# A hybrid decoder layer on one core: V projected 512 columns at a time, with a new opening

## The chip, the core and the metric

The kernel runs on one core of one Trainium2 chip. Time is device time in microseconds of that core, from the launch to the end of one execution; lower is better. The engines are TensorE (PE; its weight loads are PEld), VectorE (DVE), ScalarE (ACT), GpSimd (POOL) and SyncE (SP, which here only issues transfers). Transfers are issued from the queues of SP, ACT and POOL.

## The reference

One layer, with x of 1024 tokens by 1024 columns in float32. `h` is the RMS-normalised x; one wide product gives q, k, v (1024 columns each), u (2048) and the gates g (2048).

```python
h = rms_norm(x, attn_norm_w)
q, k, v, u, g = jnp.split(h @ w_in, splits, axis=-1)
# branch A: differential attention, 8 heads, q and k normalised, T5 bias, causal
y_a = (rms_norm(diff_attention(...), subln_w) * (1 - lam_init)) @ w_proj_attn
# branch B: GLU, causal depthwise convolution of width 31, LayerNorm, silu
c = causal_depthwise_conv(u_a * sigmoid(u_b), conv_w, conv_b)
y_b = silu(layer_norm(c, conv_ln_w, conv_ln_b)) @ w_proj_conv
x = x + (sigmoid(g_a + gate_b_a) * y_a + sigmoid(g_b + gate_b_b) * y_b) @ w_out
h = rms_norm(x, ffn_norm_w)
gt, up = jnp.split(h @ w_gate_up, 2, axis=-1)
x = x + (silu(gt) * up) @ w_down
```

## The kernel before

Every float32 operand of a large product is split into a high part (a cast on ACT, `split_hi`, L119) and a low part (a subtraction on DVE, `split_lo`, L124). A product is then three matmuls, high by high, high by low, low by high (`mm3`, L152 to L154).

**Opening.** x comes in eight tiles of 128 tokens (`xload`, L167, four buffers). The norm weights are broadcast to 128 partitions by a transfer on ACT's queue (L173). Small vectors (convolution bias, layer-norm weights, gate bias, norm weights of q and k, convolution weights, the four lambda vectors) are loaded from POOL's queue, turned by TensorE into columns of `pvec` and `cw`, and scaled (L175 to L230). `xtile` (L622) normalises one tile through `norm_T` (L606): a Square with a running sum on ACT, a reciprocal root in several small DVE operations, two multiplies of 512 columns, eight transposes on TensorE into `px`, and casts and subtractions into `hT_hi` and `hT_lo`, the transposed normalised x that all projections read.

**First phase.** The list `first` names blocks: `V` (256 columns of v), `U` (128 columns of both halves of u) and `Q` (a head's q and k). `run` asks each block's generator for one step after the other. `v_item` (L633) keeps a token tile as the stationary operand and streams 256 weight columns (`gemm_N`); two token tiles fill one bank of 512 columns, which is split and stored. In the first V block it also calls `xtile` for every tile. `u_item` (L539) keeps 128 weight columns stationary and streams 512 tokens (`gemm_T`); its four steps end in stores of the gated u. Weights are taken from a stream, `ws`, which runs two loads ahead; a raw load (`wraw`, two buffers) is split into `whi` and `wlo` (three buffers).

**Taps.** When a U block is complete, its 31 convolution taps on DVE (L519, L525) join the list `bg`. Each step of the first phase hands out 3.25 entries of that list (`TAPS_FIRST`); those that remain are spread over the 64 steps of attention, by the slack that a formula gives each step. Attention also carries the remaining Q and all G blocks on TensorE. Later stages (projections, output, the feed-forward part) are not touched.

**Order.** The program is traced in the order of the code, and a scheduler then fixes each engine's order before the launch by a simulated timeline. `after(ins)` puts the instructions of a block behind `ins` on the engine of `ins`.

Of the kernel before, what the change touches and what calls it, by code (L numbers as in the profile page):

```python
# [2 lines left out]

# [53 lines left out]
def kernel(  # L57
# [107 lines left out]
    xts = {}  # L165

    def xload(i):  # L167
        xts[i] = ap.tile([P, D], F32, tag="xt", name=f"xt{i}", bufs=4)
        nc.sync.dma_start(xts[i][:], xs[i * P : (i + 1) * P, :])

    xload(0)
    wb = ap.tile([P, D], F32, name="anw_b", bufs=1)
    nc.scalar.dma_start(wb[:], attn_norm_w.to_broadcast([P, D]))  # L173

    NROW = 64  # L175
    rows = ap.tile([NROW, P], F32, name="rows", bufs=1)
    pool.memset(rows[:], 0.0)
    col = {}
    at = [0]

    def vec_rows(key, src, n):
        r0 = at[0]
        pool.dma_start(rows[r0 : r0 + n, :], src.rearrange("o (k p) -> (o k) p", p=P))
        col[key] = r0
        at[0] += n

    vec_rows("conv_b", conv_b, 8)
    vec_rows("ln_w", conv_ln_w, 8)
    vec_rows("ln_b", conv_ln_b, 8)
    vec_rows("gate_b", gate_b, 16)  # L190
    vec_rows("subln", subln_w, 1)
    for key, src in (("qn", q_norm_w), ("kn", k_norm_w)):
        r0 = at[0]
        for j in range(2):
            pool.dma_start(rows[r0 : r0 + 1, j * HD : (j + 1) * HD], src)
        col[key] = r0
        at[0] += 1
    pvec = cst.tile([P, NROW], F32, name="pvec")
    pt = pm()
    pe.transpose(pt[:, :NROW], rows[:], ident[:NROW, :NROW])  # L200
    dve.tensor_copy(pvec[:], pt[:, :NROW])

    def pcol(key, k=0):
        c = col[key] + k
        return pvec[:, c : c + 1]

    dve.tensor_scalar(pcol("subln"), pcol("subln"), 1.0 - LAM_INIT, None, op0=ALU.mult)
    dve.tensor_scalar(pcol("kn"), pcol("kn"), -(HD ** -0.5), None, op0=ALU.mult)
    c_ = col["ln_w"]
    dve.tensor_scalar(pvec[:, c_ : c_ + 8], pvec[:, c_ : c_ + 8], -0.125, None, op0=ALU.mult)  # L210

    cwrow = ap.tile([CW, D], F32, name="cwrow", bufs=1)
    pool.dma_start(cwrow[:], conv_w[0])
    cw = cst.tile([P, NKT, 32], F32, name="cw")
    pt = pm()
    for k in range(NKT):
        pe.transpose(pt[:, k * 32 : k * 32 + CW], cwrow[:, k * P : (k + 1) * P], ident[:CW, :CW])
    dve.tensor_copy(
        cw[:, :, :CW], pt[:, : NKT * 32].rearrange("p (k t) -> p k t", t=32)[:, :, :CW]
    )  # L220

    lamt = ap.tile([P, 4, HD], F32, name="lamt", bufs=1)
    for j, src in enumerate((lam_q1, lam_k1, lam_q2, lam_k2)):
        pool.dma_start(lamt[:, j, :], src.to_broadcast([P, HD]))
    neglam = cst.tile([P, 1], F32, name="neglam")
    lprod = ap.tile([P, 2, HD], F32, name="lprod", bufs=1)
    lsum = cst.tile([P, 2], F32, name="lsum")
    for j in range(2):
        dve.tensor_tensor(lprod[:, j, :], lamt[:, 2 * j, :], lamt[:, 2 * j + 1, :], op=ALU.mult)
    dve.tensor_reduce(lsum[:], lprod[:], axis=AX.X, op=ALU.add)  # L230
# [75 lines left out]

    ws = Stream(2)

    def kt(m, k):
        return m[k] if isinstance(m, list) else m[:, k, :]  # L310

# [18 lines left out]
    v_hi = [dr.tile([S, 256], F32, name=f"v_hi{j}") for j in range(4)]  # L330
    v_lo = [dr.tile([S, 256], F32, name=f"v_lo{j}") for j in range(4)]
# [36 lines left out]

    for it in first + [x_ for l_ in later for x_ in l_]:
# [6 lines left out]
    def ld_pair(w, k, c):  # L376


        def go():
            raw = wraw()  # L380
            nc.sync.dma_start(
                raw[:].rearrange("p (k c) -> p k c", c=512),
                w[k * P : (k + 2) * P, 512 * c : 512 * (c + 1)].rearrange("(k p) c -> p k c", p=P),
            )
            hi, lo = wsplit(raw)
            return hi[:].rearrange("p (k c) -> p k c", c=512), lo[:].rearrange("p (k c) -> p k c", c=512)

        return go


    WO = ((0, (0, 1)), (1, (0,)), (1, (1,)))
    for c, _ in WO:
        ws.plan([ld_pair(wout, k, c) for k in range(0, NKT, 2)])

# [119 lines left out]
    def conv_taps(c):  # L514
# [17 lines left out]

        return [first_tap] + [tap(t) for t in range(1, CW)]

    hT_hi = big.tile([P, NKT, S], F32R, tag="xhi", name="hT_hi")
    hT_lo = big.tile([P, NKT, S], F32R, tag="xlo", name="hT_lo")


    def u_item(c):  # L539
        wb_, wa_ = ws.next(), ws.next()  # L540
        for sb in range(2):
            cs = slice(sb * 512, (sb + 1) * 512)
            ob = gemm_T(wb_, hT_hi, hT_lo, sb)
            sg = wp.tile([P, 512], F32, tag="sg", name=nm("sg"), bufs=2)
            act.activation(sg[:], ob[:], AF.Sigmoid)
            yield
            oa = gemm_T(wa_, hT_hi, hT_lo, sb)
            dve.tensor_tensor(sg[:], oa[:], sg[:], op=ALU.mult)
            nc.sync.dma_start(u_d[c][:, cs], sg[:])
            if sb == 1:  # L550
                bg.todo.insert(max(0, len(bg.todo) - CW), conv_load(c))
                bg.add(conv_taps(c))
            yield
# [52 lines left out]
    def norm_T(src, wb, hi, lo, i, junk, hbuf, tp, rstd):  # L606

        ss = sm.tile([P, 1], F32, tag="ss", name=nm("ss"))
        act.activation(junk, src, AF.Square, accum_out=ss[:])
        r = rstd(ss[:], 1.0 / D)  # L610
        for g in range(2):
            half, gs = hbuf(g), slice(512 * g, 512 * (g + 1))
            dve.scalar_tensor_tensor(half, src[:, gs], r, wb[:, gs], op0=ALU.mult, op1=ALU.mult)
# [16 lines left out]
            lambda ss, scale: rstd_of(ss, 1, scale),  # L630
        )

    def v_item(j):  # L633
        if j == 0:
            xtile(0)
        halves = [ws.next(), ws.next()]
        if j == 0:
            for i in range(1, 4):
                xload(i)
        for i2 in range(NT // 2):  # L640
            o = pg()
            for e in range(2):
                i = 2 * i2 + e
                if j == 0:
                    if i:
                        xtile(i)
                    if i + 4 < NT:
                        xload(i + 4)
                gemm_N(o[:, 256 * e : 256 * (e + 1)], halves, hT_hi, hT_lo, i)
            vh = ap.tile([P, 512], F32R, tag="vh", name=nm("vh"))  # L650
            vl = ap.tile([P, 512], F32R, tag="vl", name=nm("vl"))
            split_hi(vh[:], o[:])
            split_lo(vl[:], o[:], vh[:])
            for src, dst in ((vh, v_hi[j]), (vl, v_lo[j])):
                nc.sync.dma_start(
                    dst[256 * i2 : 256 * (i2 + 1), :].rearrange("(e p) c -> p e c", p=P),
                    f32(src[:]).rearrange("p (e c) -> p e c", c=256),
                )
            yield

    def bias_rows():
# [15 lines left out]
        pool.dma_start(t_d[h][:], b_d[h : h + 1, :].to_broadcast([P, TL]))  # L677

    qk_ctx = ExitStack()
    qkp = qk_ctx.enter_context(tc.tile_pool(name="qkp", bufs=2, side="right", reuse_waits="tile"))  # L680
    T = {}
    late = []

    def q_item(h):
        halves = [ws.next(), ws.next()]
        t = {}
        T[h] = t
# [56 lines left out]
    def run(items):  # L744
        for it in items:
            gen = MAKE[it[0]](int(it[1:]))
            while True:
# [5 lines left out]
                        late.pop(0)[1]()  # L753
                yield

    n = 0
# [25 lines left out]
    def load_v(h):  # L782
        vh = aps.tile([P, NT, VD], F32R, tag="vh", name=f"vh{h}", bufs=1)
        vl = aps.tile([P, NT, VD], F32R, tag="vl", name=f"vl{h}", bufs=1)
        for dst, src in ((vh, v_hi[h // 2]), (vl, v_lo[h // 2])):
            nc.sync.dma_start(
                f32(dst[:]),
                src[:, (h % 2) * VD : (h % 2 + 1) * VD].rearrange("(k p) d -> p k d", p=P),
            )
        V[h] = vh, vl  # L790

# [729 lines left out]
```

## Time and profile before

| | |
|---|---|
| median of three runs | 1765.96 us (1763.79 to 1766.74) |
| the profiled execution | 1767.11 us, span 1765.3 us |
| granted TensorE clock, mean | 0.998 |
| TensorE busy | 1742.3 us (99%) |
| VectorE busy | 1272.9 us (72%) |
| ScalarE busy | 801.1 us (45%) |
| first transpose of x on TensorE | at 9.35 us |
| first V block, 256-column matmuls | 11.11 us on |

Times of instructions come from the profiled execution and count from the start of its span. In a line of the profile `L152` is a line of the kernel, `out<-in` are the names of the tiles, `x64` is a count, and after `|` stand busy time in microseconds, the mean duration of one in nanoseconds, and the idle time of the engine before it with what ended it. Matmuls overlap, so their durations add up to more than the time they take. `SPq` and `ACTq` are the transfer-issuing sides of the engines.

### The profile page before, as it was taken

How to read it: one execution, taken by the hardware profiler on the slowest of the kernel's cores; microseconds unless marked ns; L12 is line 12 of the kernel's file. 1: busy time of each engine (PE TensorE's matmuls, PEld its weight loads, DVE VectorE, ACT ScalarE, POOL GpSimd, SP SyncE). 2: the span in 40 equal slices, each digit the busy share in tenths (PEclk: the TensorE clock that was granted, in tenths of full speed). 3: DMA queues.
4: the chain of work that ended last, by engine and by line, in shares of the span. 5: the costliest groups of instructions: out<-in, count | busy, mean ns of one | idle time of the engine just before them, and what ended most of it. 6: DMA issues, size and time to landing. Idle time of an engine off the chain costs nothing.

```text
span 1765.3 us, 25836 instructions
## 1 busy us (share of the span) xinstructions
PE 1742.3 (99%) x9367; PEld 1503.9 (85%) x9367; DVE 1272.9 (72%) x2187; ACT 801.1 (45%) x1886; POOL 26.6 (2%) x106
## 2 busy tenths in 40 slices
PE   7999999999999999999999999999999999999999
PEld 5898998998999998988888888878888888888887
DVE  6388888999988898886787525867667666665544
ACT  4211241558767776755557313633333333333332
POOL 3000000000000000000000000000000000000000
PEclk9999999999999999999999999999999999999999
DMA  7533354235444344352983444234544544697663
GB/s 213 197 114 110 118 143 138 72 99 147 112 134 128 90 114 142 90 159 72 338 269 103 167 167 144 90 94 157 172 150 156 178 155 140 204 355 249 215 217 130
DMA packets 255728, 275.34 MB, mean 156 GB/s; under 512 B 16064, under 2 KB 177896, under 8 KB 255600
## 3 DMA queue, kind: packets, MB, share of 16 engines
q1 hardware_dynamic: 253568, 267.45, 47.4%
q0 software_dynamic: 1744, 5.19, 1.0%
q8 instruction: 74, 1.21, 0.3%
q10 hardware_dynamic: 288, 1.05, 0.2%
q14 instruction: 54, 0.44, 0.1%
HBM read 176.59 MB, written 78.68 MB: 145 GB/s over the span
## 4 chain that ended last, share of the span: by engine, by line
PE 93%; DMA 3%; DVE 2%; ACT 1%; issue 1%; SPq 0%; DVEq 0%; ACTq 0%
PE acc L1375 19%; PE pg L152 15%; PE pg L154 15%; PE pg L153 15%; PE acc L451 12%; PE sc L817 2%; PE sc L816 2%; PE wo L154 2%; PE wo L152 2%; PE wo L153 2%; PE pT L852 2%; PE pW L152 1%; PE pW L154 1%; PE pW L153 1%; DMA xt<-in_x_dram 1%; PE pQ L714 1%
## 5 line engine op out<-in xcount | busy, mean ns | idle before, releaser
L525 DVE SCALAR_TENSOR_TENSOR acc<-u,cw,acc 128x1024 f32<-128x1024 f32 x240 | 307.1, 1280 | 2.8
L152 PE MATMUL pg<-whi,hT_hi 128*128 128x256 f32 x768 | 220.8, 288 | 0.7 <-ACT hT_hi L119 0.6
L154 PE MATMUL pg<-whi,hT_lo 128*128 128x256 f32 x768 | 220.2, 287 | 0.5 <-DVE hT_lo L124 0.2
L153 PE MATMUL pg<-wlo,hT_hi 128*128 128x256 f32 x768 | 219.5, 286 | 0.4 <-DVE wlo L124 0.4
L119 ACT CAST whi<-wraw 128x1024 fp32r<-128x1024 f32 x109 | 114.4, 1050 | 215.6 <-PE pg L153 121.5
L152 PE MATMUL pg<-hT_hi,whi 128*128 128x512 f32 x512 | 201.7, 394 | 0.0
L154 PE MATMUL pg<-hT_hi,wlo 128*128 128x512 f32 x512 | 201.0, 393 | 0.0
L153 PE MATMUL pg<-hT_lo,whi 128*128 128x512 f32 x512 | 200.6, 392 | 0.0
L124 DVE TENSOR_TENSOR wlo<-wraw,whi 128x1024 fp32r<-128x1024 f32 x109 | 133.1, 1222 | 71.0 <-ACT whi L119 66.9
L124 DVE TENSOR_TENSOR wlo<-draw,whi 128x1024 fp32r<-128x1024 f32 x75 | 91.8, 1225 | 89.3 <-ACT whi L119 84.8
L152 PEld LDWEIGHTS pg<-whi,hT_hi 128*128 128x128 f32 x768 | 148.0, 193 | 3.8 <-ACT hT_hi L119 1.4
L154 PEld LDWEIGHTS pg<-whi,hT_lo 128*128 128x128 f32 x768 | 148.0, 193 | 2.4 <-DVE hT_lo L124 0.7
L153 PEld LDWEIGHTS pg<-wlo,hT_hi 128*128 128x128 f32 x768 | 148.1, 193 | 2.2 <-DVE wlo L124 0.7
L119 ACT CAST whi<-draw 128x1024 fp32r<-128x1024 f32 x75 | 78.8, 1051 | 129.8 <-PE acc L451 119.6
L451 PE MATMUL acc<-wlo,whi 128*128 128x512 f32 x308 | 119.9, 389 | 0.0
L451 PE MATMUL acc<-whi,wlo 128*128 128x512 f32 x308 | 119.8, 389 | 0.0
L823 ACT ACTIVATE E<-E,mn 128x256 f32<-128x256 f32 (+7 forms) x128 | 99.8, 780 | 35.9 <-DVE mn L818 33.7
L154 PEld LDWEIGHTS pg<-hT_hi,wlo 128*128 128x128 f32 x512 | 96.2, 188 | 19.1
L153 PEld LDWEIGHTS pg<-hT_lo,whi 128*128 128x128 f32 x512 | 96.3, 188 | 18.5
L152 PEld LDWEIGHTS pg<-hT_hi,whi 128*128 128x128 f32 x512 | 96.3, 188 | 18.3
L1375 PE MATMUL acc<-h_lo,whi 128*128 128x512 f32 x240 | 93.4, 389 | 0.0
L1375 PE MATMUL acc<-h_hi,whi 128*128 128x512 f32 x240 | 93.4, 389 | 0.0
(270 smaller groups left out, 3957.0 us busy)
## 6 DMA issues: line engine op xcount, KB each, us to landing
wraw<-in_w_gate_up_dram SPq DMA_DIRECT2D x44, 512.0 KB, 4.8
wraw<-in_w_in_dram SPq DMA_DIRECT2D x40, 512.0 KB, 4.5
qs<-qs SPq DMA_DIRECT2D x96, 128.0 KB, 2.3
wd<-in_w_down_dram SPq DMA_DIRECT2D x44, 256.0 KB, 3.1
tdT<-wd SPq DMA_DIRECT2D x88, 128.0 KB, 4.4
draw<-sdS SPq DMA_DIRECT2D x44, 256.0 KB, 3.8
draw<-tdT SPq DMA_DIRECT2D x44, 256.0 KB, 3.7
wraw<-in_w_in_dram SPq DMA_DIRECT2D x32, 256.0 KB, 3.3
```

Of the source, the lines that this page charges most:

```text
L119: act.copy(dst, src)
L124: last_lo[0] = dve.tensor_tensor(dst, src, f32(hi), op=ALU.subtract).ins
L152: pe.matmul(o, lh, rh, start=start, stop=False)
L153: pe.matmul(o, lh, rl, start=False, stop=False)
L154: last_mm[0] = pe.matmul(o, ll, rh, start=False, stop=stop).ins
L451: m = pe.matmul(o[s_][i][:], l_[:, ts], r_[:, 512:], start=start and j + y_ == 0, stop=j == n - 1 and y_ == 2, skip_group_check=not start,)
L525: dve.scalar_tensor_tensor(acc[0][:], us[c][:, t : t + S], cw[:, c, t : t + 1], acc[0][:], op0=ALU.mult, op1=ALU.add)
L816: pe.matmul(o[:, :w], qh[:, qs], k, start=True, stop=False)
L817: last_mm[0] = pe.matmul(o[:, :w], ql[:, qs], k, start=False, stop=True).ins
L823: act.activation(e[:, :nk], e[:, :nk], AF.Exp, bias=mn[:, j : j + 1], scale=-1.0, accum_out=l[:, j : j + 1])
L852: pe.transpose(pt[:, k * P : (k + 1) * P], e[:, (k0 + k) * P : (k0 + k + 1) * P], ident[:])
L1375: pe.matmul(o[:], a_[x_][:, k, :], b_[y_][:, k, :], start=start and k + x_ + y_ == 0, stop=k == 3 and x_ == 1, skip_group_check=not start,)
```

## The change

- **V in two blocks of 512 columns.** `v_item` takes four weight pairs (two groups of 128 rows by 512 columns each), one token tile fills a bank in 24 matmuls, and each tile is stored by itself. In the first tile of the first block the matmuls are ordered by operand parts instead of by k. `v_hi` and `v_lo` become two arrays of 512 columns. V's split weights have a pool of their own (`vw`, four buffers), which is closed before the q and k pool opens.
- **A written opening.** `opening` loads the four weight pairs of the first V block among the x tiles, and then runs a list of steps: normalise a tile, split a weight pair, take a weight of the first U block. Each step's DVE instructions go behind those of the step before. Then come four V tiles, the first half of U block 0 (512 tokens), the small vectors, the other four V tiles, and the rest of U block 0.
- **Norm weights.** One row of them is loaded, and two products with a row of ones (512 columns each) spread it over the partitions; ACT copies the results out of PSUM.
- **First x tile.** It is loaded in halves from two queues; ACT squares one half and DVE the other.
- **Small vectors.** Their loads move into `vectors()`, on SP's queue, behind the last transfer traced at that point.
- Three x buffers instead of four; `bias_rows` behind the last DVE instruction traced.

```diff
     def xload(i):
-        xts[i] = ap.tile([P, D], F32, tag="xt", name=f"xt{i}", bufs=4)
+        xts[i] = ap.tile([P, D], F32, tag="xt", name=f"xt{i}", bufs=3)
         nc.sync.dma_start(xts[i][:], xs[i * P : (i + 1) * P, :])
-    xload(0)
+    xts[0] = ap.tile([P, D], F32, tag="xt", name="xt0", bufs=3)
+    nc.sync.dma_start(xts[0][:, 0:512], xs[0:P, 0:512])
+    nc.scalar.dma_start(xts[0][:, 512:1024], xs[0:P, 512:1024])
+    anw = ap.tile([CW, D], F32, tag="cwrow", name="anw_row", bufs=1)[0:1, :]
+    nc.scalar.dma_start(anw, attn_norm_w)
     wb = ap.tile([P, D], F32, name="anw_b", bufs=1)
-    nc.scalar.dma_start(wb[:], attn_norm_w.to_broadcast([P, D]))
+    one = ap.tile([1, P], F32, name="one", bufs=1)
+    pool.memset(one[:], 1.0)
+    for g in range(2):
+        pt = pm()
+        pe.matmul(pt[:], one[:], anw[:, 512 * g : 512 * (g + 1)], start=True, stop=True)
+        act.copy(wb[:, 512 * g : 512 * (g + 1)], pt[:])
...
-        pool.dma_start(rows[r0 : r0 + n, :], src.rearrange("o (k p) -> (o k) p", p=P))
+            nc.sync.dma_start(rows[r0 : r0 + n, :], src.rearrange("o (k p) -> (o k) p", p=P))
...
-    first = ["V0", "U0", "U1", "V1", "U2", "U3", "V2", "U4", "Q0", "V3", "U5", "U6", "U7"]
+    first = ["V0", "U0", "U1", "U2", "V1", "U3", "U4", "Q0", "U5", "U6", "U7"]
...
+    def vtiles():
+        return [vw.tile([P, 1024], F32R, tag=t_, name=nm(t_), bufs=4) for t_ in ("vwh", "vwl")]
...
-            return ld_wide(win, [(V0 + 256 * c, 256)])
+            return [ld_pair(win, k, V0 + 512 * c, tiles=vtiles) for k in range(0, NKT, 2)]
...
-        act.activation(junk, src, AF.Square, accum_out=ss[:])
-        r = rstd(ss[:], 1.0 / D)
+        if i:
+            act.activation(junk, src, AF.Square, accum_out=ss[:])
+            r = rstd(ss[:], 1.0 / D)
+        else:
+            s2 = sm.tile([P, 1], F32, tag="ss", name=nm("ss"))
+            act.activation(junk[:, :512], src[:, :512], AF.Square, scale=D ** -0.5, accum_out=ss[:])
+            dve.tensor_tensor_reduce(
+                junk[:, 512:], src[:, 512:], src[:, 512:], 1.0 / D, EPS, ALU.mult, ALU.add, accum_out=s2[:]
+            )
+            dve.tensor_tensor(s2[:], s2[:], ss[:], op=ALU.add)
+            r = rsq(s2[:], 1, False)
...
+    def v_item(j, w=None):
+        w = w or [ws.next() for k in range(4)]
+        for i in range(NT):
             o = pg()
...
+            ts = slice(i * P, (i + 1) * P)
+            terms = [(k, a_, b_) for k in range(NKT) for a_, b_ in ((0, 0), (0, 1), (1, 0))]
+            if i == j == 0:
+                terms.sort(key=lambda t_: (t_[2], t_[1], t_[0]))
+            for n_, (k, a_, b_) in enumerate(terms):
+                l_, r_ = (hT_hi, hT_lo)[a_][:, k, ts], w[k // 2][b_][:, k % 2, :]
+                last_mm[0] = pe.matmul(o[:], l_, r_, start=n_ == 0, stop=n_ == len(terms) - 1).ins
...
+    def opening():
+        raws = [wraw(), wraw()] + [ap.tile([P, 1024], F32, tag="vraw", name=nm("vraw"), bufs=2) for k in range(2)]
+        for k, raw in enumerate(raws):
+            nc.sync.dma_start(
+                raw[:].rearrange("p (k c) -> p k c", c=512),
+                win[2 * k * P : 2 * (k + 1) * P, V0 : V0 + 512].rearrange("(k p) c -> p k c", p=P),
+            )
+            if k in (1, 2):
+                xload(k)
...
+        for step in (
+            lambda: xtile(0), lambda: split(0), lambda: split(1), lambda: split(2), lambda: xtile(1),
+            lambda: (split(3), xload(3)), lambda: xtile(2), lambda: (xload(4), xtile(3)),
+            lambda: uw.append(ws.next()), lambda: (xload(5), xtile(4)), lambda: (xload(6), xtile(5)),
+            lambda: (xload(7), xtile(6)), lambda: xtile(7),
+        ):
+            with after(last_of(mybir.EngineType.DVE)):
+                step()
+        uw.append(ws.next())
+        v, u = v_item(0, [w[k] for k in range(4)]), u_item(0, uw)
+        for i in range(4):
+            yield next(v)
+        yield next(u)
+        with after(last_of(mybir.EngineType.SP)):
+            vectors()
+        yield next(u)
+        yield from v
+        yield from u
...
-    for _ in run(first):
+    for _ in chain(opening(), run(first[2:])):
         n += 1
         if n == 16:
-            bias_rows()
+            with after(last_of(mybir.EngineType.DVE)):
+                bias_rows()
```

More of the change, by code (lines that the diff above doesn't have):

```diff
@@ L1 @@
 import math
+from itertools import chain
 from contextlib import ExitStack, nullcontext
@@ L205, in pcol @@
         return pvec[:, c : c + 1]
[L207 to L229, printed above, removed]
@@ L230, with vectors, vec_rows @@
-    dve.tensor_reduce(lsum[:], lprod[:], axis=AX.X, op=ALU.add)
+    def vectors():
+        rows = ap.tile([NROW, P], F32, name="rows", bufs=1)
+        pool.memset(rows[:], 0.0)
+        def vec_rows(key, src, n):
+            r0 = at[0]
+            nc.sync.dma_start(rows[r0 : r0 + n, :], src.rearrange("o (k p) -> (o k) p", p=P))
+            col[key] = r0
+            at[0] += n
+        vec_rows("conv_b", conv_b, 8)
+        vec_rows("ln_w", conv_ln_w, 8)
+        vec_rows("ln_b", conv_ln_b, 8)
+        vec_rows("gate_b", gate_b, 16)
+        vec_rows("subln", subln_w, 1)
+        for key, src in (("qn", q_norm_w), ("kn", k_norm_w)):
+            r0 = at[0]
+            for j in range(2):
+                nc.sync.dma_start(rows[r0 : r0 + 1, j * HD : (j + 1) * HD], src)
+            col[key] = r0
+            at[0] += 1
+        cwrow = ap.tile([CW, D], F32, tag="cwrow", name="cwrow", bufs=1)
+        nc.sync.dma_start(cwrow[:], conv_w[0])
+        lamt = ap.tile([P, 4, HD], F32, name="lamt", bufs=1)
+        for j, src in enumerate((lam_q1, lam_k1, lam_q2, lam_k2)):
+            nc.sync.dma_start(lamt[:, j, :], src.to_broadcast([P, HD]))
+        pt = pm()
+        pe.transpose(pt[:, :NROW], rows[:], ident[:NROW, :NROW])
+        dve.tensor_copy(pvec[:], pt[:, :NROW])
+        dve.tensor_scalar(pcol("subln"), pcol("subln"), 1.0 - LAM_INIT, None, op0=ALU.mult)
+        dve.tensor_scalar(pcol("kn"), pcol("kn"), -(HD ** -0.5), None, op0=ALU.mult)
+        c_ = col["ln_w"]
+        dve.tensor_scalar(pvec[:, c_ : c_ + 8], pvec[:, c_ : c_ + 8], -0.125, None, op0=ALU.mult)
+        pt = pm()
+        for k in range(NKT):
+            pe.transpose(pt[:, k * 32 : k * 32 + CW], cwrow[:, k * P : (k + 1) * P], ident[:CW, :CW])
+        dve.tensor_copy(
+            cw[:, :, :CW], pt[:, : NKT * 32].rearrange("p (k t) -> p k t", t=32)[:, :, :CW]
+        )
+        lprod = ap.tile([P, 2, HD], F32, name="lprod", bufs=1)
+        for j in range(2):
+            dve.tensor_tensor(lprod[:, j, :], lamt[:, 2 * j, :], lamt[:, 2 * j + 1, :], op=ALU.mult)
+        dve.tensor_reduce(lsum[:], lprod[:], axis=AX.X, op=ALU.add)
@@ L327, in gemm_N @@
             mm3(o, kt(shi, k)[:, ts], kt(slo, k)[:, ts], whi[:, k % 4, :], wlo[:, k % 4, :], k == 0, k == NKT - 1)
-    v_hi = [dr.tile([S, 256], F32, name=f"v_hi{j}") for j in range(4)]
-    v_lo = [dr.tile([S, 256], F32, name=f"v_lo{j}") for j in range(4)]
+    v_hi = [dr.tile([S, 512], F32, name=f"v_hi{j}") for j in range(2)]
+    v_lo = [dr.tile([S, 512], F32, name=f"v_lo{j}") for j in range(2)]
     a_d = [dr.tile([P, S], F32, name=f"a_d{h}") for h in range(H)]
@@ L367, in loads_of @@
         return ld_cols(win, G0 + c * P)
-    for it in first + [x_ for l_ in later for x_ in l_]:
+    for it in first[1:] + [x_ for l_ in later for x_ in l_]:
         ws.plan(loads_of(it))
@@ L374 @@
         ws.plan(ld_cols(wpc, c * P))
[L376 to L388, printed above, removed]
     WO = ((0, (0, 1)), (1, (0,)), (1, (1,)))
     for c, _ in WO:
-        ws.plan([ld_pair(wout, k, c) for k in range(0, NKT, 2)])
+        ws.plan([ld_pair(wout, k, 512 * c) for k in range(0, NKT, 2)])
     SEVEN = (
@@ L679, with qk_pool @@
     qk_ctx = ExitStack()
-    qkp = qk_ctx.enter_context(tc.tile_pool(name="qkp", bufs=2, side="right", reuse_waits="tile"))
     T = {}
     late = []
+    pools = {}
+    def qk_pool():
+        if not pools:
+            vw_ctx.close()
+            pools["qk"] = qk_ctx.enter_context(tc.tile_pool(name="qkp", bufs=2, side="right", reuse_waits="tile"))
+        return pools["qk"]
     def q_item(h):
+        qkp = qk_pool()
         halves = [ws.next(), ws.next()]
```

69 lines of the change are left out of this document (25 added, 44 removed).

## The prediction

> **What bounds the kernel now.** I read the page first: busy shares and the chain that ended last.
>
> ```profile
> span 1765.3 us, 25836 instructions
> PE 1742.3 (99%) x9367; PEld 1503.9 (85%) x9367; DVE 1272.9 (72%) x2187; ACT 801.1 (45%) x1886; POOL 26.6 (2%) x106
> PE 93%; DMA 3%; DVE 2%; ACT 1%; issue 1%; SPq 0%; DVEq 0%; ACTq 0%
> ```
>
> TensorE is busy in all but 23 us of the span, and the chain runs through it. So an edit pays only if it makes matmuls cheaper, removes TensorE's waits, or lifts a period in which its busy time is slow. The waits of TensorE say where the idle time lies:
>
> ```profile
> PE px L616 <- DVE xt L613: 9.3, 1, 9.3
> PE px L616 <- issue: 1.5, 1, 1.5
> ```
>
> Over a third of all idle time is the wait for the first normalised half tile of x. The other large entry is also a transpose of x. So next the windows of the opening (columns: start and end, length, busy time and count of PE, PEld, DVE, ACT, POOL, then the granted clock, DMA share, GB/s):
>
> ```profile
> 0.00:9.35 9.35, 0.00 (x0) 0.03 (x1) 1.80 (x8) 2.79 (x5) 5.58 (x16) 1.00 0.84 213
> 9.35:20.00 10.65, 8.08 (x40) 6.38 (x40) 8.05 (x23) 8.06 (x15) 3.91 (x10) 1.00 0.97 336
> 20.00:23.00 3.00, 2.83 (x15) 2.43 (x16) 2.81 (x7) 1.82 (x5) 0.00 (x0) 0.56 0.68 212
> 23.00:27.30 4.30, 4.30 (x23) 4.30 (x22) 4.17 (x23) 1.94 (x4) 0.00 (x0) 0.52 0.44 128
> 29.50:39.00 9.50, 9.15 (x68) 7.93 (x69) 6.14 (x17) 4.60 (x10) 1.14 (x3) 1.00 0.48 164
> ```
>
> Idle is 9.35, 2.57, 0.17 and 0.35 us in the first, second, third and last row. The fourth row is "busy" throughout, at half the clock: 23 instructions in 4.3 us, where the last has 68 in 9.5. Busy time alone hides part of the loss, so I count work at its steady pace. Two pure stretches give the pace, the first of 512-column matmuls (U blocks), the second of 256-column ones (a V block):
>
> ```profile
> 120.00:162.00 42.00, 42.00 (x187) 34.77 (x186) 35.97 (x32) 6.63 (x9) 0.12 (x1) 1.00 0.35 111
> 163.09:186.00 22.91, 22.91 (x192) 22.91 (x191) 20.83 (x20) 3.86 (x5) 0.00 (x0) 1.00 0.31 105
> ```
>
> A matmul lasts 0.39 us in the records but its successor starts earlier, so a window also counts the one or two still ending at its left edge: 185 starts in 42.00 us are 0.227 us each. The second window runs from a first start to a last start: 22.91/191 = 0.120 us.
>
> TensorE's work from the start to 96.51 us, where the second V block begins, by form:
>
> ```profile
> L152 PE MATMUL pg<-hT_hi,whi 128*128 128x512 f32 x64 | 25.0, 391 | 0.0
> L154 PE MATMUL pg<-hT_hi,wlo 128*128 128x512 f32 x64 | 24.8, 390 | 0.0
> L153 PE MATMUL pg<-hT_lo,whi 128*128 128x512 f32 x64 | 24.8, 390 | 0.0
> L152 PE MATMUL pg<-whi,hT_hi 128*128 128x256 f32 x65 | 20.8, 319 | 0.7 <-ACT hT_hi L119 0.6
> L154 PE MATMUL pg<-whi,hT_lo 128*128 128x256 f32 x64 | 20.1, 314 | 0.5 <-DVE hT_lo L124 0.2 <-DVE v L603 0.2
> L153 PE MATMUL pg<-wlo,hT_hi 128*128 128x256 f32 x64 | 19.6, 306 | 0.4 <-DVE wlo L124 0.4
> L616 PE MATMUL px<-ident,xt 128*128 128x128 f32 x64 | 10.9, 301 | 10.9 <-DVE xt L613 9.3 <-issue 1.5
> L672 PE MATMUL pm<-oh,rb 33*8 33x384 f32 x6 | 2.3, 484 | 0.0
> L217 PE MATMUL pm<-ident,cwrow 31*128 31x31 f32 x8 | 1.1, 291 | 0.0
> ```
>
> ```profile
> 45.95 0.88 PE px L616 x8
> ```
>
> The last row, from the chain, gives 0.11 us per transpose. Steady work: 192 x 0.227 = 43.6, 192 x 0.120 = 23.0, 64 x 0.11 = 7.0, 2.3 and 1.1, together 77.0 us. The opening therefore loses 96.5 - 77.0 = 19.5 us: 12.4 idle, 7.1 at a low clock or stretched.
>
> **V's width.** Before, V is four blocks of 192 matmuls of 256 columns: 768 x 0.120 = 92.2 us. After, two blocks of 192 of 512 columns: 384 x 0.227 = 87.2 us. Gain 5.0 us, all on the path, since TensorE is the bound there. Evictions (32 of 512 columns), stores (256 KB each) and weight loads (512 KB each) keep their number. In the Trainium skill, "TensorE: Matmul & The Clock Gate", section "Back-to-back issue gap", the gap is columns over 2.4 GHz plus about 2.5 ns, so that a pair of 256s costs 218.4 ns against 215.8 and the edit would be worth only about 1.0 us, an estimate; the two windows show 240 against 227, so I keep 5.0.
>
> **The opening.** Rows for its chain, from the timeline:
>
> ```profile
> 0.74 0.39 SPq L169 DMA_DIRECT2D xt<-in_x_dram  x1
> 0.77 0.39 ACTq L173 DMA_DIRECT2D anw_b<-in_attn_norm_w_dram  x1
> 5.92 1.06 ACT L609 ACTIVATE xj<-xt 128x1024 f32<-128x1024 f32 x1 [3.90 <-DMA xt<-in_x_dram]
> 7.10 0.15 DVE L603 TENSOR_SCALAR v<-ss 128x1 f32<-128x1 f32 x1 [7.10 <-ACT xj L609]
> 8.49 1.42 DVE L613 SCALAR_TENSOR_TENSOR xt<-xt,r,anw_b 128x512 f32<-128x512 f32 x2
> ```
>
> The bytes in half-microsecond slices of the first 20 us, and what single instructions of this stretch take:
>
> ```profile
> GB/s 0 0 0 106 106 164 328 434 401 336 314 410 369 258 277 83 85 161 214 215 269 386 392 422 427 388 364 402 403 403 363 367 383 327 238 345 335 300 200 157
> ```
>
> ```profile
> L124 DVE TENSOR_TENSOR hT_lo<-px,hT_hi 128x512 fp32r<-128x512 f32 x16 | 10.9, 686 | 9.0 <-ACT hT_hi L119 8.9
> L124 DVE TENSOR_TENSOR wlo<-wraw,whi 128x1024 fp32r<-128x1024 f32 x4 | 4.9, 1225 | 3.3 <-ACT whi L119 3.3
> ```
>
> ```profile
> L119 ACT CAST hT_hi<-px 128x512 fp32r<-128x512 f32 x16 | 9.2, 583 | 12.7 <-PE px L616 12.7
> ```
>
> The spread of the norm weights by DMA moves 0.52 MB beside the first x tile. Without it that tile should land about 0.52 MB / 400 GB/s = 1.3 us earlier, at 4.6. The halved Square saves some 0.5 of the 2.57 us from 5.92 to 8.49: the multiply at 6.7. Its weights must be there too: one row, then a product with ones and a copy for each half. The nearest product is the 384-column one of L672, 2.3/6 = 0.39 us, so 0.5 us at 512 columns, about twice that at half clock, and 0.58 for the copy: first half at 6.5 to 7.0. I let the multiply start at 6.8, against 8.49. These two products cost 0.9 us of TensorE (0 to 2).
>
> From there VectorE's order is what binds: each step of the new opening queues its VectorE instructions behind the step before. A tile takes 1.39 from v to the multiply (7.10 to 8.49), 1.42 for both halves, then for the second half four transposes 0.5, cast 0.58, lo 0.69, and about 0.35 of hand-overs: 4.9 us. Tile 0 ends at 10.3 (10.7 with slow transposes); three weight splits of 1.225 at 14.4; tile 1 at 19.4; the fourth split at 20.6; tiles 2 and 3 at 25.6 and 30.6. Weights and x tiles 1 and 2 are 3.7 MB with tile 0; at 390 GB/s from 3 us they are in by 13.4, ahead of their splits. The dip to 83 to 215 GB/s from 7.5 to 10 us coincides with the small vectors, which now come later.
>
> TensorE: by 19.0 it can have done 22 matmuls of tile 0 (5.0), 16 transposes (1.8) and the products (0.9): 7.7, so 11.3 lost. Having waited, it starts at about half clock, as the rows at 20 to 27 show; 3.4 us of that cost 1.7. Then it is fed: tile 1 and the rest of tile 0 last to 26.6, tile 2 has been ready since 25.6, each further tile asks 0.9 + 24 x 0.227 = 6.3 us where VectorE needs 4.9. After four tiles VectorE also does three weight splits, of which the third waits for a buffer and its load; U's first block (48 x 0.227 = 10.9 us) covers this stretch until tile 4 at about 42, while TensorE is at about 50. Loss 13.0, or 15.0 if a tile takes 6 us on VectorE; I take 13.6. Net of the 0.9: 19.5 - 13.6 - 0.9 = 5.0 us gained (0 to 7; 0 if VectorE's strict order and the later second half cost as much as the missing transfer gives).
>
> **Small vectors.** Their 14 transfers move from POOL's queue to SP's, behind the store of U's first block, at 0.39 us an issue 5.5 us of SP. Behind them queue V's stores and the next weight loads. U's second half block, and V tiles already split, keep TensorE fed for more than 10 us; price 0, at most 3 if the transposes of these rows stand early in TensorE's order and their rows come late. The first use of the convolution weights is far behind. Three x buffers for four: tile 3 now waits for tile 0's transposes, 8 us, and is needed at 25.6: nothing.
>
> **Taps.** VectorE's convolution taps are handed out 3.25 per yield once U block 0 is complete: yield 8 of 52 before, 12 now. So 4 x 3.25 = 13 taps move into attention:
>
> ```profile
> 82.00:396.00 314.00, 190.83 (x149) 1.00 0.37 112
> 396.00:845.00 449.00, 116.28 (x91) 1.00 0.42 119
> ```
>
> That is 13 x 1.278 = 16.6 us more VectorE work in attention. What VectorE carries there:
>
> ```profile
> 396.00:845.00 449.00, 446.42 (x2973) 406.66 (x2972) 383.27 (x906) 309.69 (x1059) 10.58 (x59) 1.00 0.42 119
> 396.00:450.00 54.00, 52.95 (x372) 48.32 (x371) 49.09 (x121) 41.75 (x154) 1.57 (x9) 1.00 0.50 142
> 450.00:500.00 50.00, 50.00 (x346) 46.16 (x345) 46.48 (x117) 40.04 (x152) 1.08 (x6) 1.00 0.40 107
> ```
>
> It rises from 85% to 89%. At 93% TensorE idles not at all (450 to 500); at 91% 1.05 us in 54 (396 to 450), which over 449 us would be 8.7 against the 2.6 now: +6.1. Price 0 to 6.1, and 16.6 if nothing is absorbed; I take 2.0, nearer the row without idle time, as most of attention has none.
>
> **Sum.** -5.0 - 5.0 + 2.0 = -8.0 us. The profiled execution took 1767.1 us (span 1765.3 and 1.8 around it), 1.1 over the median; by it 1759.1. Against the median, 1765.96 - 8.0 = 1758.0.
>
> **Rivals.**
> 1. *The opening gives nothing* (0 for 5.0): 1765.96 - 5.0 + 2.0 = 1763.0. For it: VectorE is serialised and the first tile's matmuls now need 2 MB of weights, not 1. Against: 12.4 us of idle time and 0.52 MB are in reach.
> 2. *VectorE binds in attention*: the 13 taps end up on the path, 16.6 us, 1765.96 - 10.0 + 16.6 = 1772.6, slower. It decides from about 10 us, eight taps not absorbed. For it: 91% with idle time at 396 to 450. Against: 93% without, and 66 us of VectorE idle there.
> 3. *The wide matmul saves only the issue gap*, 1.0 for 5.0: 1765.96 - 1.0 - 5.0 + 2.0 = 1762.0; the page of the Trainium skill named above gives this rule. The two pace windows speak against it, though the wide ones there are not V's own.
> 4. *All taps absorbed, opening at its best* (7.0): 1765.96 - 12.0 = 1754.0.
>
> **Numbers.** Forecast 0.60, rivals 0.16, 0.12, 0.04, 0.08. A measurement of this kernel tells about 0.2%, 3.5 us, from no change. Faster: forecast, 4, 3: 0.72; within: rival 1: 0.16; slower: rival 2: 0.12. The range goes from 1753 (a little under rival 4) to 1767 (opening nothing and 6.1 of attention): it leaves out rival 2 and a tail.
>
> **What would show it.** V's matmuls of 512 columns at 0.227 from start to start; first transpose of x at about 7.5 instead of 9.35; the start of V tile 2 at 26 to 28; no TensorE wait between 30 and 100; 13 fewer taps before attention and TensorE idle there 3 to 8 us. Wrong if a wide V matmul takes 0.24, if TensorE waits over 3 us behind the fourth weight split or tile 4, or if attention is over 5 us longer.

## The result, and the profile after

| | before | after |
|---|---|---|
| median, us | 1765.47 | 1791.51 |
| ratio | | 1.0146 (1.0133 to 1.0159) |
| profiled execution, span | 1765.3 | 1789.3 |

The change makes the kernel 26 us slower; 8 us faster was forecast. The page of the kernel after:

```profile
span 1789.3 us, 25085 instructions
PE 1753.9 (98%) x8987; PEld 1490.4 (83%) x8987; DVE 1271.3 (71%) x2189; ACT 804.0 (45%) x1890; POOL 19.6 (1%) x93
PE 90%; DVE 4%; DMA 3%; ACT 2%; issue 1%; SPq 0%; ACTq 0%; DVEq 0%
```

TensorE does 380 instructions fewer: 384 wide matmuls stand for 768, and the products with ones add four. But it is idle for 35.4 us instead of 23.0, and VectorE has 4% of the chain instead of 2%. The waits of TensorE, longest first:

```profile
PE pm L236 <- DMA cwrow<-in_conv_w_dram: 6.1, 1, 6.1
PE pm L183 <- DMA anw_row<-in_attn_norm_w_dram: 4.4, 1, 4.4
PE pg L673 <- ACT hT_hi L120: 3.6, 6, 2.0
PE px L645 <- DVE xt L642: 2.7, 2, 2.4
PE sc L883 <- DVE mn L885: 2.6, 3, 1.0
```

To place the rest, split the run in three: to the first score, from there to the first projection matmul (attention), and what follows. The rows of those two tiles give the borders (first and last start), before and then after:

```profile
L816 PE MATMUL sc<-ks,qs x192: 220/389/501, 321.2 to 815.3; 128*128 128x512 f32 x96, 128*128 128x128 f32 x32, 128*128 128x256 f32 x32, 128*128 128x384 f32 x32
L152 PE MATMUL pg<-aTh,whi x128: 387/389/799, 849.3 to 940.6; 128*128 128x512 f32 x128
```

```profile
L883 PE MATMUL sc<-ks,qs x192: 220/389/792, 329.4 to 833.5; 128*128 128x512 f32 x96, 128*128 128x128 f32 x32, 128*128 128x256 f32 x32, 128*128 128x384 f32 x32
L153 PE MATMUL pg<-aTh,whi x128: 387/389/799, 872.0 to 964.3; 128*128 128x512 f32 x128
```

The first phase is 8.2 us longer (329.4 - 321.2), attention 14.5 (542.6 against 528.1), the rest 1.3. (The prediction let attention begin at 396 us; its first score is at 321.2.) I use the prediction's measure again: the loss at a time is that time less the matmuls started so far, each at its steady pace. The losses below are counted from the starts in the traces.

| loss, us, at | 41 us | 55 us | 100 us | first score | first projection |
|---|---|---|---|---|---|
| before | 19.7 | 19.7 | 19.7 | 19.6 | 27.0 |
| after | 19.3 | 19.5 | 30.7 | 31.0 | 52.9 |

To 55 us nothing is gained and nothing lost. Between 55 and 100 us 11 us are lost. The shorter V then takes back 3.2 (5.0 for its width, less 1.8 for the products with ones), and attention loses 14.5 more than before.

**From 55 to 100 us.** Windows of the kernel after:

```profile
60.00:65.00 5.00, 0.07 (x1) 0.07 (x2) 0.00 (x0) 0.00 (x0) 0.00 (x0) 0.83 0.41 142
65.00:70.00 5.00, 5.00 (x18) 4.07 (x19) 3.69 (x16) 1.15 (x2) 0.00 (x0) 0.50 0.17 62
70.00:75.00 5.00, 4.71 (x25) 3.81 (x24) 0.70 (x2) 1.32 (x3) 0.00 (x0) 0.98 0.00 0
```

In the first row all five engines stand still. In the second TensorE is busy at half the clock (0.50). The transfer queue of SP and TensorE's timeline say why:

```profile
52.45 0.35 SPq L205 DMA_DIRECT2D rows<-in_conv_b_dram  x1
...
57.43 0.25 SPq L221 DMA_DIRECT2D cwrow<-in_conv_w_dram  x1
...
59.54 0.43 SPq L224 DMA_DIRECT2D lamt<-in_lam_k_dram  x1
```

```profile
64.93 1.05 PE L236 MATMUL pm<-ident,cwrow 31*128 31x31 f32 x8 [6.14 <-DMA cwrow<-in_conv_w_dram]
74.81 0.50 PE L673 MATMUL pg<-vwh,hT_hi 128*128 128x512 f32 x1 [0.29 <-ACT hT_hi L120]
82.14 0.50 PE L673 MATMUL pg<-vwh,hT_hi 128*128 128x512 f32 x1 [0.33 <-ACT hT_hi L120]
89.48 0.50 PE L673 MATMUL pg<-vwh,hT_hi 128*128 128x512 f32 x1 [0.33 <-ACT hT_hi L120]
```

The 14 small loads take 7.5 us of SP's queue. The convolution weights are issued at 57.43 and TensorE can turn them at 64.93; the transposes stand ahead of U's second half in its fixed order, so everything behind them waits, the next x tiles included. The last three rows show V tiles at 7.3 us apiece, where the steady pace asks 6.3 (24 matmuls and eight transposes), so 1 us is lost on each.

**The end of attention.** Four windows of the kernel before, then the same stretch, shifted by 23 us, of the kernel after:

```profile
797.00:807.00 10.00, 10.00 (x56) 8.58 (x55) 8.39 (x21) 6.78 (x18) 0.36 (x2) 1.00 0.36 119
807.00:817.00 10.00, 10.00 (x50) 8.25 (x49) 9.24 (x20) 5.64 (x14) 0.00 (x0) 1.00 0.20 80
817.00:827.00 10.00, 9.24 (x66) 7.87 (x64) 5.16 (x8) 6.38 (x16) 0.56 (x3) 1.00 0.25 79
827.00:837.00 10.00, 10.00 (x46) 8.24 (x45) 2.07 (x6) 2.34 (x10) 0.00 (x0) 1.00 0.07 28
```

```profile
820.00:830.00 10.00, 9.02 (x52) 7.18 (x50) 9.50 (x23) 6.90 (x18) 0.36 (x2) 1.00 0.41 133
830.00:840.00 10.00, 7.59 (x30) 5.59 (x30) 10.00 (x21) 6.00 (x15) 0.36 (x2) 0.66 0.03 12
840.00:850.00 10.00, 9.01 (x45) 8.26 (x46) 4.07 (x8) 3.74 (x11) 0.20 (x1) 0.66 0.10 41
850.00:860.00 10.00, 10.00 (x46) 8.25 (x45) 2.07 (x6) 2.32 (x9) 0.00 (x0) 1.00 0.08 28
```

At 830 to 840 VectorE (third busy figure) has no free moment, TensorE starts 30 instructions in 10 us and its clock falls to 0.66. The chain in order of time shows what VectorE is doing there:

```profile
830.85 0.80 DVE pl L125 x2
831.65 1.19 DVE acc L542
832.84 0.60 DVE E L885
833.52 0.59 DVE E L885
834.18 0.46 issue
834.64 1.28 DVE acc L542
835.92 0.33 DVE pl L125
836.25 0.66 DVE E L885
837.05 0.66 DVE E L885
837.72 1.20 DVE acc L542
838.91 1.06 DVE E L899
```

`acc L542` are taps. Between the score steps of the last head they lie on the path itself. At the steady pace attention would take 520.7 us; what it takes above that is called its loss. Its last tenth is the stretch that holds the last tenth of this steady work. Of the 21.9 us that attention loses in all, 12.3 fall in its last tenth; before it is 2.8 of 7.4.

### The profile page after: what moved, and what is told of

It is laid out like the page before. It is cut to its first block, busy times and chain, and to the rows that moved or that the text cites. A ratio compares the mean times of both kernels' runs of the same rounds, so it can differ in the third digit from the quotient of the medians.

```text
span 1789.3 us, 25085 instructions
## 1 busy us (share of the span) xinstructions
PE 1753.9 (98%) x8987; PEld 1490.4 (83%) x8987; DVE 1271.3 (71%) x2189; ACT 804.0 (45%) x1890; POOL 19.6 (1%) x93
## 4 chain that ended last, share of the span: by engine, by line
PE 90%; DVE 4%; DMA 3%; ACT 2%; issue 1%; SPq 0%; ACTq 0%; DVEq 0%
PE acc L1442 21%; PE pg L153 13%; PE pg L154 13%; PE pg L155 13%; PE acc L468 12%; PE pg L673 5%; PE sc L884 2%; PE wo L155 2%; PE wo L154 2%; PE wo L153 2%; PE sc L883 2%; PE pT L919 1%; PE pW L153 1%; DMA wraw<-in_w_in_dram 1%; PE pW L155 1%
## 5 line engine op out<-in xcount | busy, mean ns | idle before, releaser
L542 DVE SCALAR_TENSOR_TENSOR acc<-u,cw,acc 128x1024 f32<-128x1024 f32 x240 | 306.7, 1278 | 2.5
L120 ACT CAST whi<-wraw 128x1024 fp32r<-128x1024 f32 x101 | 106.2, 1052 | 188.0 <-PE pg L154 96.5
L125 DVE TENSOR_TENSOR wlo<-wraw,whi 128x1024 fp32r<-128x1024 f32 x101 | 123.1, 1220 | 75.1 <-ACT whi L120 74.8
L153 PE MATMUL pg<-whi,hT_hi 128*128 128x256 f32 x512 | 146.3, 286 | 0.0
L154 PE MATMUL pg<-wlo,hT_hi 128*128 128x256 f32 x512 | 145.8, 285 | 0.0
L155 PE MATMUL pg<-whi,hT_lo 128*128 128x256 f32 x512 | 145.7, 285 | 0.0
L153 PEld LDWEIGHTS pg<-hT_hi,whi 128*128 128x128 f32 x512 | 96.2, 188 | 21.6 <-ACT sgg L580 2.8
L153 PEld LDWEIGHTS pg<-whi,hT_hi 128*128 128x128 f32 x512 | 97.6, 191 | 2.1 <-ACT jk L728 0.5
L154 PEld LDWEIGHTS pg<-wlo,hT_hi 128*128 128x128 f32 x512 | 97.6, 191 | 1.4
L155 PEld LDWEIGHTS pg<-whi,hT_lo 128*128 128x128 f32 x512 | 97.6, 191 | 0.9
```

The source lines that it names most:

```text
L120: act.copy(dst, src)
L125: last_lo[0] = dve.tensor_tensor(dst, src, f32(hi), op=ALU.subtract).ins
L153: pe.matmul(o, lh, rh, start=start, stop=False)
L154: pe.matmul(o, lh, rl, start=False, stop=False)
L155: last_mm[0] = pe.matmul(o, ll, rh, start=False, stop=stop).ins
L542: dve.scalar_tensor_tensor(acc[0][:], us[c][:, t : t + S], cw[:, c, t : t + 1], acc[0][:], op0=ALU.mult, op1=ALU.add)
```

## The experiments

In each, time is given as ratio to the kernel before on the same chip, with the interval, and as median.

**Taps handed out as before, in the changed kernel.**

```diff
-    TAPS_FIRST = 3.25
+    TAPS_FIRST = 3.57
```

> The changed kernel with 3.57 taps per yield instead of 3.25, so that 41 yields hand out the 146 entries that 45 yields did before. Theory T (the 13 taps moved into attention put VectorE on its path): attention, from the first score to the first projection matmul, falls from 542.6 us to about 528, and the time from 1791.5 to about 1777. Rival R (attention is longer for another reason, such as V's new rows in memory or another instruction order): attention stays within 3 us of 542.6 and the time at 1789 to 1794.

1776.17, ratio 1.0060 (1.0045 to 1.0075). Attention takes 530.0 us (327.0 to 857.0). By the times the taps account for 15 us; in the profiles 12.6 of them lie in attention.

**Fewer taps, in the kernel before.**

```diff
-    TAPS_FIRST = 3.25
+    TAPS_FIRST = 2.95
```

> The kernel before with 2.95 taps per yield instead of 3.25, so that 45 yields hand out 133 entries as in the changed kernel; nothing else of the change. Theory T: attention grows from 528.1 us to about 542, the time from 1765.5 to about 1780. Rival R: 1765 to 1769.

1778.22, ratio 1.0072 (1.0057 to 1.0087), 12 us slower; attention 540.3. Most of the loss comes with nothing else of the change, and VectorE is full at the same place, but the place holds less of it: of the 12.2 us that attention takes more than before, 5.5 fall in its last tenth, against 9.5 of 14.5 in the changed kernel. Its window there:

```profile
817.00:827.00 10.00, 5.99 (x31) 4.99 (x30) 9.96 (x21) 6.76 (x15) 0.00 (x0) 0.87 0.37 131
```

The kernel with 3.57 taps has executed as many taps by its first score as this one (119, counted in the trace), and yet its attention is 10 us shorter. So where the taps stand in VectorE's order counts, not only how many are left. Rival R is out.

**Small vectors loaded early, from POOL.**

```diff
-            nc.sync.dma_start(rows[...], ...)   # in vectors(), behind U's first half
+        pool.dma_start(rows[...], ...)          # at the start; the transposes stay
```

> The changed kernel with the 14 loads of the small vectors issued from POOL's queue at the start, as before; their transposes stay behind U's first half block. Theory W (TensorE waits for the late convolution weights and then runs cold): the 6.1 us wait and the 2.6 us at half clock after it go, 1791.5 falls to about 1783. Rival N (the next late thing takes its place: the x tiles come one by one from VectorE): at most 3 us gained, 1788 to 1791; and if the early loads slow the x tiles down, some of it is lost again.

1781.71, ratio 1.0092 (1.0077 to 1.0107): 9.8 us gained, as theory W has it. The loss at 100 us is 23.9 instead of 30.7, and the first score comes 6.7 us earlier (322.7).

**Only the convolution weights' load split.**

```diff
-        nc.sync.dma_start(cwrow[:], conv_w[0])
+        nc.sync.dma_start(cwrow[0:16, :], conv_w[0, 0:16])
+        nc.sync.dma_start(cwrow[16:CW, :], conv_w[0, 16:CW])
```

> The changed kernel with the load of the convolution weights split in two, 16 rows and 15 rows, both still late and on SP's queue. Its 31 rows of 4 KB were moved one after another, 0.16 us each, from 58.3 to 64 us. Theory K (31 rows go to one engine, 16 and 15 rows to as many engines as rows): TensorE's wait of 6.1 us falls to 1 to 3 us, and the time from 1791.5 to 1784 to 1788, part of the 9.8 us that the early load gave. Rival (the queue of 14 late transfers is the cause, whatever their form): the wait stays above 5 us and the time within 2 us of 1791.5.

1781.77, ratio 1.0091 (1.0075 to 1.0106), as much as the early load gave, and more than expected. The wait is gone from the list (its first 120 us):

```profile
PE pm L183 <- DMA anw_row<-in_attn_norm_w_dram: 4.8, 1, 4.8
PE px L646 <- DVE xt L643: 3.5, 3, 2.4
PE pg L674 <- ACT hT_hi L120: 3.2, 5, 1.9
PE px L646 <- issue: 0.8, 1, 0.8
```

Between 55 and 100 us this run loses 3.2 us instead of 11. So it was the form of one transfer, not the queue of 14. The packets in the traces show it: in the changed kernel the first ten rows of 4 KB move one after another, each starting when the one before has ended, from 58.33 to 60.58 us; here 16 rows start between 56.22 and 56.42 and the other 15 between 56.68 and 56.96. The Trainium skill, "DMA: Bandwidth & Descriptors", section "Why a DMA increments its semaphore by 16 and not by 1", says that a transfer uses the largest number of engines up to 16 that divides its outer dimension, which is 1 for 31 rows, 16 for 16 and 15 for 15; the two runs agree with that.

**V as pairs of 256 columns in the changed kernel.**

```diff
+            for e in range(2):
+                cs = slice(256 * e, 256 * (e + 1))
...
-                last_mm[0] = pe.matmul(o[:], l_, r_, ...)
+                    last_mm[0] = pe.matmul(o[:, cs], l_, r_[..., cs], ...)
```

> The changed kernel with each V matmul of 512 columns issued as two of 256 into the two halves of the bank. If the pace of the profile holds (0.120 against 0.227), 384 x 0.013 = 5.0 us more, 1796.5. If only the issue gap counts, 1.0 us more, 1792.5. If the first tiles wait for VectorE anyway, part of it is hidden: 1793 to 1795.

1793.26, ratio 1.0155 (1.0138 to 1.0172): 1.8 us more, in the band of the third expectation, that part of the saving is hidden. The pace itself is as predicted: in the changed kernel the wide V matmuls of the second block, with a few of U, start 0.226 us apart (178 counted in 40 us, less one that is still ending at the left edge):

```profile
150.00:190.00 40.00, 40.00 (x178) 33.14 (x177) 37.02 (x34) 4.59 (x7) 0.13 (x1) 1.00 0.70 234
```

The 192 matmuls of that block alone start from 152.04 to 195.34, 0.227 apart; in this run the same block in halves has 384 from 151.56 to 197.52, 0.120 apart. So rival 3, that only an issue gap is saved, is out for the pace. In this run's trace the loss at the first score is 28.1 instead of 31.0, so 2.9 of the 5.0 us replaced waiting. By the times alone the width would be worth 1.8 us here, but the intervals of the two ratios overlap and also allow 0, 1.0 or 5.0.

**Both repairs.** 3.57 taps and the early loads together.

> The changed kernel with both repairs: 3.57 taps per yield and the small vectors loaded early from POOL's queue. If the two causes are independent, 1791.5 - 15.3 - 9.8 = about 1766.4, the time before. If they share a cause (both merely shift work in the first phase), the second brings less than half of its own: 1771 or more.

1770.19, ratio 1.0031 (1.0022 to 1.0040). 21.3 of the 26 us are back, of 25.1 if the two simply added. This lies between the two expectations: the second repair brings over half of its own, but not all.

**And the broadcast of the norm weights as before.**

```diff
-    for g in range(2):
-        pt = pm()
-        pe.matmul(pt[:], one[:], anw[...], start=True, stop=True)
-        act.copy(wb[...], pt[:])
+    nc.scalar.dma_start(wb[:], attn_norm_w.to_broadcast([P, D]))
```

> As the kernel with both repairs, and with the norm weights spread by the broadcast transfer as before, in place of the products with ones. Theory P (the products and their copies, queued behind a weight cast on ScalarE, hold the first multiply until 9.67 us): the first transpose comes at 8.5 to 9.5 instead of 10.6, and the time falls 1 to 3 us. Rival: the transfer of 0.5 MB delays the first x tile by as much, and the order of steps on VectorE binds anyway: within 1 us.

1769.75, ratio 1.0026 (1.0016 to 1.0035), 0.4 us less. The first transpose does come earlier, at 9.05 instead of 11.2 us, but the loss at 41 us is 20.1 against 19.2. The second half of the rival holds: something else bound the opening.

**No order of steps on VectorE.** Both repairs, and

```diff
-            with after(last_of(mybir.EngineType.DVE)):
-                step()
+            step()
```

> The changed kernel with both repairs (3.57 taps per yield, small vectors loaded early from POOL) and without the order of steps on VectorE in the opening; 1770.2 with that order. Theory S (the strict order is why the opening gained nothing: 20 us lost by 40 us, as before the change): 2 to 5 us less, 1765 to 1768. Rival (the first V tile's 2 MB of weights and the width are the bound): 1769 to 1772, or more if VectorE then takes the later weight splits first.

1766.68, ratio 1.0004 (0.9993 to 1.0014): 3.5 us less, the time that theory S gives. The last transpose of x ends at 68.4 instead of 81.0. Where the gain lies is not shown: in the profile the loss at 41 us is 21.6 against 19.2, the first phase is no shorter (321.2 against 321.3) and attention is 2.4 us longer. That execution took 1771.7 us, the most of this kernel's ten.

**V's width alone, on the kernel before**, with 3.57 and with 3.25 taps per yield: `v_item` streams 512 columns from weight pairs, still calling `xtile` for each tile.

> The kernel before with only V's width changed (two blocks of 512 columns from weight pairs, the opening and the small vectors as before, x tiles normalised inside the first V block) and 3.57 taps per yield to keep the taps of the first phase. If the width is worth its pace, 1766 - 5 = 1761. If the first V block, which needs four weight pairs before its first tile is complete, gives part of it back in the opening: 1763 to 1767.

> The same with 3.25 taps per yield: U's first block is complete at yield 12 instead of 8, as in the changed kernel, so 13 taps move into attention. By the theory of the taps 12 to 15 us slower than with 3.57; if the taps only matter together with the new opening, within 3 us of it.

1765.47, ratio 1.0001 (0.9992 to 1.0011), and 1777.50, ratio 1.0061 (1.0046 to 1.0076). The taps cost 12 us again. With them put right the width gives nothing that the times show, although the first score comes at 315.0 and the matmuls before it are 5.0 us shorter. Attention takes 2.7 us longer (530.8). The opening may lose more as well: 18.4 to 21.8 us in three runs with a wide first V block, 16.4 to 20.1 in five with a narrow one; the two overlap, so this is not shown.

**Half of V wide, after the opening.** Two blocks of 256 in their old places, then one of 512; U's first block complete at yield 8.

> The kernel before with the first 512 columns of V as two blocks of 256, in their old places, and the last 512 as one wide block in the place of the third; opening, small vectors, taps (U's first block complete at yield 8, 3.25 per yield) as before. If the pace is all, 192 x 0.013 = 2.5 us less, about 1762.4. If the wide block, which needs four weight pairs while the stream runs two ahead, makes TensorE wait: within 1 us of 1764.9 or above.

1767.27, ratio 1.0006 (0.9997 to 1.0015). Its first phase is 2.0 us shorter in the profile, its attention 3.0 longer, with the same taps. Why attention gives back the gain is not settled.

**More taps before attention, kernel before**: `TAPS_FIRST = 3.5`.

> The kernel before with 3.5 taps per yield, 11 more taps before attention. Theory T, read the other way: attention loses about 7.4 us before the change, and some of it is VectorE's load; with 14 us less of it 2 to 4 us are gained, 1761 to 1763. Rival (VectorE is full in the first phase, so that the taps start later than they are handed out): within 1.5 us of 1764.9.

1766.65, ratio 1.0007 (0.9998 to 1.0015); attention 528.9. The time is the rival's: 91 instead of 102 taps handed out in attention bring nothing. Its reason holds in part: of the 11 taps that are handed out earlier only 5 more are executed by the first score (131 against 126).

**Place or amount.** No taps in the last eight attention steps, on four kernels:

```diff
-    slack[-2:] = [0.0, 0.0]
+    slack[-8:] = [0.0] * 8
```

> The changed kernel with no taps handed out in the last eight attention steps (the last head) instead of the last two; the same number of taps, spread over the 56 steps before. Theory L (place: in the last 50 us of attention TensorE waits for a chain with taps in it and then runs cold, about 10 us more than before the change): 8 to 12 us less, 1780 to 1784. Theory M (amount: VectorE is full all through attention): the taps cost the same elsewhere, within 3 us of 1791.5.

> The kernel before with the same edit. It loses 2.7 us in the last 50 us of attention. Theory L: at most those 2 to 3 us gained, 1763 to 1765. Theory M: 1766 to 1769, since the same taps crowd the other steps.

> V's width alone on the kernel before, 3.57 taps per yield, no taps in the last eight steps; without the last edit it measured the same as before (1765.5). If the 5.0 us of the pace are given back at the end of attention: 1761 to 1763. If they are given back in its middle: 1765 to 1768.

> The changed kernel with 3.57 taps per yield, early small vectors, no strict order of steps on VectorE, and no taps in the last eight steps: everything that was found, undone or mended, with V's width and the norm weights' products kept. It measured 1766.7 without the last edit. By theory L 1764 to 1766; by theory M 1767 to 1769.

| | with the edit | ratio | loss in attention, without and with | in its last tenth, without and with |
|---|---|---|---|---|
| changed kernel | 1782.61 | 1.0097 (1.0084 to 1.0111) | 21.9, 15.6 | 12.3, 2.5 |
| kernel before | 1771.02 | 1.0034 (1.0022 to 1.0047) | 7.4, 14.0 | 2.8, 3.2 |
| V wide, 3.57 taps | 1778.29 | 1.0073 (1.0060 to 1.0085) | 10.0, 22.1 | 2.4, 4.1 |
| repairs, no step order | 1774.19 | 1.0047 (1.0034 to 1.0061) | 12.6, 17.8 | 2.3, 2.9 |

Neither theory holds alone. In the changed kernel the edit takes 9.8 us out of the last tenth, as theory L has it, and adds 3.5 elsewhere. Where the last tenth was not overfull, the same taps pushed into the other steps cost attention 5 to 12 us, the way theory M has it, and these three kernels came out slower than either theory had forecast. In the kernel before, attention takes 102 handed-out taps at their old spacing with a loss of 7.4 us; 13 more cost 12 to 14.5 of their 16.6 us, and the same number at a closer spacing 5 to 12. Between 102 and 115 taps nothing was measured.

No kernel tried beats the one before; four can't be told from it (V wide with 3.57 taps, no step order, half of V wide, and 3.5 taps).

## Why the prediction was wrong

In the profiles the change costs 24.0 us: -5.0 for V's width in the matmuls, 1.8 for the products with ones, 11.4 of other loss before the first score (nearly all between 55 and 100 us), 14.5 in attention and 1.3 behind it. Term by term:

- **V's width, -5.0: right in the matmuls, not in the time.** The pace is 0.227 us as predicted. Alone on the kernel before the time did not move: the prediction took for granted that what leaves the matmuls of the first phase reaches the end. In the profile 2.7 us of it came back in attention. That execution was 2.6 us under its kernel's median, so where the rest went stays open.
- **The opening, -5.0: wrong.** The loss at 41 us is 19.3, where the step had 13.6 in all. Two terms were mis-sized. The products with ones: the row of L672 has six records for three products, so one product of 384 columns is two records and the 512-column estimate should have been double; here the four records take

```profile
4.45 3.75 PE L183 MATMUL pm<-anw_row,one 1*128 1x512 f32 x4 [4.45 <-DMA anw_row<-in_attn_norm_w_dram]
```

  instead of 0.9 to 1.8 us, and ScalarE casts a weight pair before it copies them. The multiply starts at 9.67, not 6.8. And a tile on VectorE: 4.9 us was worked out from VectorE's own operations, but its last ones wait for other engines:

```profile
18.16 0.15 DVE L623 TENSOR_SCALAR v<-ss 128x1 f32<-128x1 f32 x1
...
23.74 1.29 DVE L125 TENSOR_TENSOR hT_lo<-px,hT_hi 128x512 fp32r<-128x512 f32 x2 [2.79 <-ACT hT_hi L120]
...
26.08 0.14 DVE L623 TENSOR_SCALAR v<-ss 128x1 f32<-128x1 f32 x1
...
33.78 1.28 DVE L125 TENSOR_TENSOR hT_lo<-px,hT_hi 128x512 fp32r<-128x512 f32 x2
```

  6.9 us for tile 1 and 9.0 for tile 2. What they wait for stands in the order of the other two engines:

```profile
22.18 1.04 ACT L120 CAST whi<-wraw 128x1024 fp32r<-128x1024 f32 x1 [1.32 <-DMA wraw<-in_w_in_dram]
23.13 1.07 ACT L120 CAST hT_hi<-px 128x512 fp32r<-128x512 f32 x2
...
32.13 0.39 PE L673 MATMUL pg<-vwh,hT_lo 128*128 128x512 f32 x1
32.36 1.03 PE L645 MATMUL px<-ident,xt 128*128 128x128 f32 x8
```

  Tile 1's casts stand on ScalarE behind the cast of a weight of U that waits for its load. Tile 2's transposes stand on TensorE behind the V matmuls of tile 1. A smaller term was also too low: the step charged 3.4 us at half clock after the first wait, where its own rows show about half clock from 20.00 to 27.30; in the kernel after, the granted clock is 0.50 from 22.4 to 29.2. Rival 1, that the opening gives nothing, came out in this part, but its reasons are not shown: the loss at 41 us was no smaller in the profile without VectorE's strict order, and the larger need of weights was not tried by itself.
- **Small vectors, priced at 0, at most 3: wrong.** 9.8 us hung on them. The step looked at when the result is first used, and named the danger (transposes early in TensorE's order, rows late), but it priced only the issues, at 0.39 us each, and not how long one transfer takes: the 31 rows on SP's queue held their transposes until 7.5 us after their issue. It also left out the clock after the wait.
- **Taps, +2.0: wrong.** The 13 taps were right as handed out (12 fewer were executed by the first score), but the price was 14.5 us of attention, near the upper bound of 16.6. The step took VectorE's mean share as the measure of room, over 396 to 845 us. Over attention as it is (321.2 to 849.3 before, 329.4 to 872.0 after) VectorE is busy for 453 of 528 us and for 465 of 543: 86% both times, while the stage grew by 14.5. The share of a stage says nothing on its last steps, where 9.5 of the 14.5 us were lost. Rival 2 named the mechanism; its 1772.6 had the opening's gain in it.
- The range ended at 1767 because it left out rival 2, and it held no case in which two terms fail together.

## What to carry to other kernels

When an edit delays the first item of a background job that is handed out by steps, count what is pushed into the next stage and look at that stage's last steps, not at its mean load: 13 operations of 1.28 us cost 12 to 14.5 us in a stage where VectorE was 86% busy. A load that moves later needs its own transfer's duration priced in its new queue and form, together with the place of its consumer in the in-order queue. A faster pace on the bounding engine need not reach the end: here 5.0 us fewer of matmuls left the time as it was. So measure the width edit by itself first.

## What the runs showed of the hardware

- A load of 31 rows of 4 KB on SP's queue took from its issue at 57.43 to 64.93 before its consumer ran; as 16 and 15 rows, issued at 55.27 and 55.63, they were there when their consumer's turn came at 58.34.
- After a wait of 6 us TensorE's granted clock was 0.50 for the next 5 us; in the last steps of attention (830 to 850) it was 0.66 without a single wait over 1.5 us.
- Five kernels with the same opening lost 16.4 to 20.1 us by the first score, one profile each, so a single profile can't settle a difference of 2 us there.
